# Delta-rule values of a hybrid decoder layer: from channels to tokens by VectorE in squares of 32 and two transfers through DRAM, in place of TensorE transposes

## The chip, the core and the metric

The kernel runs on one core of a Trainium2 chip. The metric is the device time of one execution in microseconds (us), lower is better. Three runs of the kernel before gave 1606.45, 1606.53 and 1606.76 us; their median is 1606.53 us.

Engines in the profile: PE is TensorE, PEld its weight loads, DVE VectorE, ACT ScalarE, POOL GpSimd, SP SyncE. Each engine has one queue that it works off in order; SP issues nearly all DMAs and, being in order as well, stands still while the first DMA in its queue waits for something.

## The reference

One layer for 512 tokens and 1024 channels, all float32: half of a SwiGLU block is added, then a mixer, then half of a second SwiGLU block. The mixer projects its input once and feeds two recurrent branches; the change lies in one of them, the gated delta rule with 8 key heads and 16 value heads:

```python
qkv = jax.nn.silu(causal_short_conv(jnp.concatenate([gq, gk, gv], axis=-1), conv_w))
cq, ck, cv = jnp.split(qkv, [GDN_WIDTH_K, 2 * GDN_WIDTH_K], axis=-1)
...
T = lax.linalg.triangular_solve(eye + A, ...)          # a triangle per chunk and head
u = jnp.matmul(T, v * beta[..., None])
...
v_new = u_c - jnp.einsum('bhtk,bhkv->bhtv', w_c, S)
```

The short convolution runs along the tokens, so it wants a channel per partition and tokens along the free dimension. The chunked rule wants tokens on the partitions: its products sum over tokens, and `beta` is a factor per token. So the values `cv` of each of the 16 value heads, 128 channels by 512 tokens, have to be turned once.

## The kernel before

The span has three stages: the first SwiGLU block (to about 357 us), the mixer (to about 1192 us), the second block and the last norm. All dense products are made on PE with operands split in a high and a low part, three products per tile (`mm3`, L189 to L191). Each 256-KB piece of weights (a slab) comes in by one SP load into one of 3 `raw` buffers; ACT casts the high part (L1754), DVE subtracts for the low part (L1756) and then one of 6 pairs of buffers `whi`, `wlo` holds it until PE has used it.

The mixer is laid down by a planner (`Desk`, L64). Every piece of work is a generator that asks for an engine with an estimated duration (`V`, `A`, `T_`, `S` for DVE, ACT, PE, SP), for a buffer (`get`), for an event (`on`) or lets time pass (`lag`, with the due times of `LAG`). The planner replays these estimates and so decides in which order instructions stand in each engine's queue; on the chip that order is fixed and only semaphores count. The dense products are a thread of their own that fills PE; products of the recurrences get PE in between. PSUM has two accumulators "mm" for dense results, and lanes: "a" and "b" with two buffers, "d" and "e" with one.

What the change and the prediction touch:

- `conv` (L1091): takes two of the six `ta` buffers, drains a dense result from "mm" into `ci` (L1097), works out four taps (ACT L1102, three times DVE L1105) and tanh (ACT L1108); a last DVE instruction (L1113) writes the silu. For q and k the result goes to its tile in another view (n is not 0). For the values (n is 0) it goes to the tile `gvb` or `x` of the head, channels on partitions. Then both `ta` buffers come free.
- `g_w` (L1244): waits for the head's values and its factors, takes lane "e", turns the tile by four PE transposes into PSUM (`ptv`, L1251), and DVE multiplies them by a factor per token on the way back into the same tile (L1253).
- `g_rec` (L1333): the recurrence of a unit, that is of two value heads with one key head, in four chunks of 128 tokens: `pks` (L1374, L1375), DVE adds the value (L1378), `pw` (L1387), DVE (L1392), `pog` (L1401, L1403), DVE updates the state (L1410, L1414).
- `g_b`, a step for each unit: sends diagonal blocks to DRAM (`nb`, four issues, L1222), reads them back spread out (`gfs`, four issues of 128 KB, L1228), loads a start matrix (`hmask`, L1234), and POOL solves small triangles with them (L1240, L1241).
- The inverse of a unit continues on PE, ACT and DVE (`pq`, L1289 to L1320, DVE stream transposes L1265, L1272, L1329), the triangle itself comes from `pgq` (L1189, with DVE L1193 and L1195), the turned output is `pto` (L1445, DVE L1449).
- `loader` (L1696): SP's weight loads. It asks `choose` for the next projection, and where nothing can be loaded yet it asks again after 0.5 us of planned SP time (L1702).

The two loops over the units: 8 units, each with two value heads, so 16 heads v0 to v15, 64 transposes and 16 multiplies.

Of the kernel before, what the change touches and what calls it, by code (L numbers as in the profile page):

```python
# [8 lines left out]
F32 = mybir.dt.float32  # L9
# [3 lines left out]
ALU = mybir.AluOpType  # L13
# [3 lines left out]
P = 128  # L17
T = 512
NT = T // P
D = 1024  # L20
# [28 lines left out]
STAY = (15,)  # L49
CONVS = 7  # L50
SLACK = 0.8
LAG = dict(raw=3.5, gb=6.5, nb=6, m=7, out=5, back=6)
EASE = 2.5
LANES = {"a": 2, "b": 2, "d": 1, "e": 1}

# [632 lines left out]
def mixer(tc, mp, e):  # L688
    nc = tc.nc
    pe, act, dve, pool, sp = nc.tensor, nc.scalar, nc.vector, nc.gpsimd, nc.sync  # L690
    cs, ident, tri, strict, hm, ones, mhalf = (e[k] for k in ("cs", "ident", "tri", "strict", "hm", "ones", "mhalf"))
    uh, ul, rbc, rcols, rcol, rhalf, h = (e[k] for k in ("uh", "ul", "rbc", "rcols", "rcol", "rhalf", "h"))
    psc, dr, dense, slab, wp, mm3, ux, hd, dbg = (
        e[k] for k in ("psc", "dr", "dense", "slab", "wp", "mm3", "ux", "hd", "dbg"))
    wt, wn, wab, wbh, wbg, wo, dta, psd = (e[k] for k in ("wt", "wn", "wab", "wbh", "wbg", "wo", "dtab", "psd"))

    def ps(name, lane="d"):
        return psc.tile([P, T], F32, tag="p" + lane, name=name, bufs=LANES[lane])

    def v3(ap, a):  # L700
        return ap.rearrange("p (a b) -> p a b", a=a)

    def bc(ap, n):

        return ap.unsqueeze(2).to_broadcast([ap.shape[0], ap.shape[1], n])
# [9 lines left out]
    op = [alloc(f"op{i}", 1) for i in range(8)]  # L715
    ta = alloc("ta", TA)
# [3 lines left out]
    for size, names in ((1024, "n2:2 gz:2 fs:1 ut:1"), (512, "kn:3 gm:1 qm:2 gb:2 ln:1 at:4 vb:4 t64:2 on:2"),  # L720
                        (256, "ft:1 tp:1 thg:2 x:1 we:1 s:3 w:1"), (128, "fm:1"), (64, "sm:4")):
        for it in names.split():
            n, b = it.split(":")
# [35 lines left out]
    D = Desk(wx0=1, wx1=1, wx2=1, wx3=1, mm=2, a=2, b=2, d=1, e=1, ta=TA, tm=6, thg=1, raw=RB, w=WB, n2=2, gz=2, fs=1, ut=1, t=3, kn=3, gm=1,  # L759
             qm=2, gb=2, ln=1, mi=3, mt=3, at=4, vb=4, t64=2, on=2, ft=1, x=1, we=1, w_=1, s=3)  # L760
    V = lambda n: ("use", "DVE", 0.21 + 0.001 * n)
    A = lambda n: ("use", "ACT", 0.2 + 0.0009 * n)
    T_ = lambda n: ("use", "PE", n)
    S = ("use", "SP", 0.4)
# [11 lines left out]
    def decays(pab):  # L776
# [74 lines left out]
        sp.dma_start(gtd, gt)  # L851
        yield "lag", LAG["out"]
        D.fire("decays")
# [237 lines left out]
    def conv(k, i, pt, out, n):  # L1091

        yield "get", "ta", 2
        yield *V(512), 1
        ci = ta("ci", (P, T + 32))[:, :T + 3]
        dve.memset(ci[:, :3], 0.0)
        dve.tensor_tensor(ci[:, 3:], pt, rbc, op=ALU.mult)  # L1097
        D.put("mm")
        wc = [cs[:, C_CV + 4 * i + j:C_CV + 4 * i + j + 1] for j in range(4)]
        yield A(512)  # L1100
        y = ta("cy")
        act.activation(y, ci[:, :T], AF.Copy, scale=wc[0])  # L1102
        for j in range(1, 4):
            yield V(550)
            dve.scalar_tensor_tensor(y, ci[:, j:j + T], wc[j], y, op0=ALU.mult, op1=ALU.add)  # L1105
        yield A(512)
        th = ci[:, :T]
        act.activation(th, y, AF.Tanh, scale=0.5)  # L1108
        a, b = (v3(th, n), v3(y, n)) if n else (th, y)
        if k[0] in "qk" and k[1] > 3:  # L1110
            yield "on", ("K", k[1] - 4)
        yield V(512)
        dve.scalar_tensor_tensor(out, a, 1.0, b, op0=ALU.add, op1=ALU.mult)  # L1113
        D.put("ta", 2)
        D.fire(k)

    def g_e(u, st):

# [2 lines left out]
        for i in range(2):  # L1121
# [4 lines left out]
            act.dma_start(gb, gtd[hd_:hd_ + 1].rearrange("o (c b) -> o c b", c=NT).to_broadcast([P, NT, P]))  # L1126
            yield "lag", LAG["gb"]
            a = G["at"][u % 4 * 2 + i]
# [85 lines left out]
    def g_b(u, st):  # L1214
# [4 lines left out]
        for b in range(4):  # L1219
            r = slice(32 * b, 32 * b + 32)  # L1220
            yield S
            sp.dma_start(nb[b].rearrange("s i j -> i s j"), n2[r, :, :, r].rearrange("p a c j -> p (a c) j"))  # L1222
        yield "lag", LAG["nb"]
        yield "on", *([("P", u - 1)] if u else ["m"])
# [9 lines left out]
        sp.dma_start(t, eye4)  # L1234
        yield "lag", LAG["m"]
        for j in range(31):
# [6 lines left out]

    def g_w(u, i, st):  # L1244
        yield "on", ("v", 2 * u + i), ("C", u)
        yield "get", "e", 1
        vb = G["vb"][u % 3 * 2 + i]
        yield T_(Patient(.5))
        pt = ps("ptv", "e")
        for c in range(NT):  # L1250
            pe.transpose(pt[:, c * P:(c + 1) * P], vb[:, c], ident)  # L1251
        yield V(512)
        dve.tensor_tensor(vb, v3(pt, NT), bc(st["c2"][:, :, i], P), op=ALU.mult)  # L1253
        D.put("e")
        D.fire(("W", u, i))

    def g_inv(u, st):
# [75 lines left out]
    def g_rec(u, st):  # L1333
        yield "on", ("I", u), ("W", u, 0), ("W", u, 1), ("N", u), *([("R", u - 2)] if u > 1 else []), \
            *(["more"] if u else [("x", 0), ("we", 0), ("w", 0)])
        kq, kn, at, ut, sm = (st[k] for k in ("kq", "kn", "at", "ut", "sm"))
        vb = G["vb"][u % 3 * 2:u % 3 * 2 + 2]
        hd2 = [slice(i * P, (i + 1) * P) for i in range(2)]
        we, w, x = (G[n][u % 2] for n in ("we", "w", "x"))
        s = None  # L1340
# [27 lines left out]
        for c in range(NT):  # L1368
            pk = None
            if c > 0:  # L1370
                yield "get", "a", 1
                yield T_(.88)
                pk = ps("pks", "a")
                pe.matmul(pk[:, :256], kq[:, c, 0], s, start=True, stop=True)  # L1374
                pe.matmul(pk[:, 256:], kq[:, c, 1], s, start=True, stop=True)  # L1375
                for i in range(2):
                    yield V(150)
                    dve.scalar_tensor_tensor(x[:, hd2[i]], pk[:, hd2[i]], st["c1"][:, c, i:i + 1], vb[i][:, c],  # L1378
                                             op0=ALU.mult, op1=ALU.add)
                xs = [x[:, :P], x[:, P:]]  # L1380
            else:
                xs = [vb[0][:, c], vb[1][:, c]]
            yield "get", "b", 1
            yield T_(.46)
            pw = ps("pw", "b")
            for i in range(2):
                pe.matmul(pw[:, hd2[i]], ut[:, 4 * i + c], xs[i], start=True, stop=True)  # L1387
            D.start((2, u, c, 0), values(c, pw))
            if c < NT - 1:
                for i in range(2):  # L1390
                    yield V(150)
                    dve.tensor_scalar(we[:, hd2[i]], pw[:, hd2[i]], ek[:, c, 2 * u + i:2 * u + i + 1], None,  # L1392
                                      op0=ALU.mult)
            yield "on", ("w", u, c)
            D.put("b")

            yield "get", "b", 1
            yield T_(.9)
            po = ps("pog", "b")
            if c < NT - 1:  # L1400
                pe.matmul(po[:, :256], kn[:, c], we, start=True, stop=True)  # L1401
            for i in range(2):
                pe.matmul(po[:, 256 + i * P:256 + (i + 1) * P], at[i][:, c], w[:, hd2[i]], start=True, stop=True)  # L1403
            D.start((2, u, c, 1), outputs(c, po, pk))
            if c < NT - 1:
                yield "get", "s", 1
                s2 = places["s"]("s", (P, 256))
                if c == 0:
                    yield V(256)
                    dve.tensor_copy(s2, po[:, :256])  # L1410
                else:
                    for i in range(2):
                        yield V(150)
                        dve.scalar_tensor_tensor(s2[:, hd2[i]], s[:, hd2[i]], eend[:, c, 2 * u + i:2 * u + i + 1],  # L1414
                                                 po[:, hd2[i]], op0=ALU.mult, op1=ALU.add)
                    D.put("s")
                s = s2
                D.fire(("s", u, c))
# [8 lines left out]
                                 op0=ALU.mult, op1=ALU.add)  # L1427
# [12 lines left out]
        for i in range(2):  # L1440
            yield "get", "b", 1
            yield T_(Patient(.5))
            pt = ps("pto", "b")
# [9 lines left out]
            if u == 7:  # L1453
# [3 lines left out]
                a, b = so[k] = uh[:, k - 8], ul[:, k - 8]  # L1457
# [158 lines left out]
    G = {"kq": [hv[:, i].rearrange("p (c a b) -> p c a b", c=NT, a=2) for i in range(3)]}  # L1616
    st = [{} for _ in range(8)]
# [78 lines left out]
    def loader():  # L1696
        n = 0
        while todo or gates:
            yield "get", "raw", 1
            x = choose()  # L1700
            while x is None:
                yield "use", "SP", 0.5  # L1702
                x = choose()
            line.append(x)
            D.fire(("f", x))
            D.fire(("line", len(line)))
            for q, src in enumerate(weights(*x)):
                if q:
                    yield "get", "raw", 1
                yield S  # L1710
                raw = wp.tile([P, 512], F32, tag="raw", name="raw", bufs=RB)
                sp.dma_start(raw, src)
                D.start((1, n), maker((x, q), raw))
                n += 1
        for d, q in wbgs:
            yield "get", "raw", 1
            yield S
            raw = wp.tile([P, 512], F32, tag="raw", name="raw", bufs=RB)
            sp.dma_start(raw, wbg[d][:, q * 512:(q + 1) * 512])
            D.start((1, n), maker((("m", d), q), raw))  # L1720
            n += 1
# [175 lines left out]
    for d in range(8):  # L1897
        hr = ta("hr")
        sp.dma_start(hr, hd[d])
        pt = dense(wo[d], KD, lambda k: ms[k])  # L1900
# [78 lines left out]
```

## Time and profile before

| | |
|---|---|
| median of 3 runs | 1606.53 us |
| the profiled execution's span | 1604.7 us |
| median less span | 1.8 us |
| DVE busy | 1145.7 us (71%) |
| ACT busy | 831.0 us (52%) |
| POOL busy | 408.8 us (25%) |
| DMA | 204.91 MB, mean 128 GB/s |
| granted PE clock, 640 to 1060 us | 1.00 |

The profiled execution's own time isn't listed apart from its span; about 1.8 us lie around the span if it ran like the median. A group's row gives the line, engine, operation, out<-in with the shapes, its count, then busy time in us and the mean of one in ns, then the idle time just before it and what ended it. A timeline row gives start and length in us. PE's records overlap: a dense product is shown with 0.39 us, yet the next starts 0.23 us later. So PE's work is read from starts, not from lengths.

### The profile page before, as it was taken

How to read it: one execution, taken by the hardware profiler on the slowest of the kernel's cores; microseconds unless marked ns; L12 is line 12 of the kernel's file. 1: busy time of each engine (PE TensorE's matmuls, PEld its weight loads, DVE VectorE, ACT ScalarE, POOL GpSimd, SP SyncE). 2: the span in 40 equal slices, each digit the busy share in tenths (PEclk: the TensorE clock that was granted, in tenths of full speed). 3: DMA queues.
4: the chain of work that ended last, by engine and by line, in shares of the span. 5: the costliest groups of instructions: out<-in, count | busy, mean ns of one | idle time of the engine just before them, and what ended most of it. 6: DMA issues, size and time to landing. Idle time of an engine off the chain costs nothing.

```text
span 1604.7 us, 29242 instructions
## 1 busy us (share of the span) xinstructions
PE 1593.7 (99%) x10672; PEld 1386.3 (86%) x10672; DVE 1145.7 (71%) x2259; ACT 831.0 (52%) x1872; POOL 408.8 (25%) x725
## 2 busy tenths in 40 slices
PE   9999999999999999999999999999999999999997
PEld 8999998888888888888888888888888899999887
DVE  6888785447787778668788888765545788878433
ACT  5766674332434345456665665554324666667222
POOL 0211212001221221156545556600001121121001
PEclk9999999999999999999999999999999999999998
DMA  5766863332312322443242334445543586686333
GB/s 187 168 162 156 181 160 103 113 117 86 106 47 68 86 92 87 137 135 104 93 125 80 119 107 129 134 136 186 164 142 128 140 183 158 154 187 146 92 91 117
DMA packets 121824, 204.91 MB, mean 128 GB/s; under 512 B 21184, under 2 KB 27072, under 8 KB 121680
## 3 DMA queue, kind: packets, MB, share of 16 engines
q1 hardware_dynamic: 104688, 172.40, 34.3%
q0 software_dynamic: 14400, 26.22, 10.2%
q10 hardware_dynamic: 2592, 4.42, 1.0%
q8 instruction: 84, 1.38, 0.4%
q14 instruction: 60, 0.49, 0.1%
HBM read 188.02 MB, written 14.97 MB: 126 GB/s over the span
## 4 chain that ended last, share of the span: by engine, by line
PE 91%; DMA 3%; issue 3%; DVE 2%; ACT 0%; POOL 0%; POOLq 0%; SPq 0%; DVEq 0%; ACTq 0%
PE pmm L189 19%; PE pmm L191 19%; PE pmm L190 19%; PE px L191 6%; PE px L190 6%; PE px L189 6%; DMA wlo<-w1a 2%; PE pnat L189 2%; PE pnat L191 2%; PE pnat L190 2%; PE pgq L1189 1%; PE pw L1387 1%; PE pog L1403 1%; PE pl L974 1%; PE pd L917 1%
## 5 line engine op out<-in xcount | busy, mean ns | idle before, releaser
L189 PE MATMUL pmm<-uh,whi 128*128 128x512 f32 x879 | 361.3, 411 | 0.0
L191 PE MATMUL pmm<-uh,wlo 128*128 128x512 f32 x879 | 343.0, 390 | 0.0
L190 PE MATMUL pmm<-ul,whi 128*128 128x512 f32 x879 | 341.9, 389 | 0.0
L191 PE MATMUL px<-xs,wlo 128*128 128x256 f32 x1008 | 285.7, 283 | 1.3 <-DMA wlo<-w1a 0.7
L190 PE MATMUL px<-xs,whi 128*128 128x256 f32 x1008 | 285.2, 283 | 0.0
L189 PE MATMUL px<-xs,whi 128*128 128x256 f32 x1008 | 285.2, 283 | 0.0
L1754 ACT CAST whi<-raw 128x512 fp32r<-128x512 f32 x226 | 140.2, 621 | 242.7 <-PE pmm L190 195.2
L1756 DVE TENSOR_TENSOR wlo<-raw,whi 128x512 fp32r<-128x512 f32 x226 | 158.3, 702 | 118.2 <-ACT whi L1754 116.2
L191 PEld LDWEIGHTS pmm<-uh,wlo 128*128 128x128 f32 x879 | 165.0, 188 | 36.1 <-DVE wlo L607 0.2
L191 PEld LDWEIGHTS px<-xs,wlo 128*128 128x128 f32 x1008 | 193.5, 192 | 2.1 <-DMA wlo<-w1a 1.1
L189 PEld LDWEIGHTS px<-xs,whi 128*128 128x128 f32 x1008 | 193.5, 192 | 0.1
L190 PEld LDWEIGHTS px<-xs,whi 128*128 128x128 f32 x1008 | 193.5, 192 | 0.1
L189 PEld LDWEIGHTS pmm<-uh,whi 128*128 128x128 f32 x879 | 165.5, 188 | 30.4
L190 PEld LDWEIGHTS pmm<-ul,whi 128*128 128x128 f32 x879 | 165.7, 189 | 29.5 <-DVE ul L216 0.2
L329 ACT CAST whi<-sw 128x512 fp32r<-128x512 f32 x144 | 87.6, 613 | 92.8 <-DVE sw L366 72.6
L308 DVE TENSOR_TENSOR wlo<-raw,whi 128x512 fp32r<-128x512 f32 x100 | 77.7, 788 | 76.7 <-ACT whi L329 76.3
L329 ACT CAST whi<-raw 128x512 fp32r<-128x512 f32 x104 | 61.2, 592 | 125.6 <-PE pmm L190 92.8
L227 POOL TENSOR_TENSOR acc<-acc,sqt 128x512 f32<-128x512 f32 x18 | 23.4, 1302 | 319.8 <-ACT sqt L225 319.8
L308 DVE TENSOR_TENSOR wlo<-sw,whi 128x512 fp32r<-128x512 f32 x144 | 98.0, 681 | 0.0
L329 ACT CAST whi<-rw 128x512 fp32r<-128x512 f32 (+1 forms) x130 | 79.6, 613 | 26.6 <-PE px L190 13.4
L190 PE MATMUL pmm<-xs,whi 128*128 128x512 f32 (+1 forms) x238 | 89.7, 377 | 0.1
L189 PE MATMUL pmm<-xs,whi 128*128 128x512 f32 (+1 forms) x238 | 89.8, 377 | 0.0
(476 smaller groups left out, 3223.5 us busy)
## 6 DMA issues: line engine op xcount, KB each, us to landing
raw<-wt SPq DMA_DIRECT2D x160, 256.0 KB
rw<-w1b SPq DMA_DIRECT2D x80, 256.0 KB
rw<-w1a SPq DMA_DIRECT2D x74, 256.0 KB
wlo<-w1b POOLq DMA_DIRECT2D x53, 256.0 KB, 4.8
wlo<-w1a POOLq DMA_DIRECT2D x47, 256.0 KB, 5.0
raw<-w2b SPq DMA_DIRECT2D x41, 256.0 KB
raw<-w2a SPq DMA_DIRECT2D x36, 256.0 KB
raw<-wn SPq DMA_DIRECT2D x32, 256.0 KB
```

Source lines behind the costliest of these rows:

```text
L189: pe.matmul(pt, ah, bh, start=first, stop=False)
L190: pe.matmul(pt, ah, bl, start=False, stop=False)
L191: pe.matmul(pt, al, bh, start=False, stop=last)
L227: add.tensor_tensor(acc, acc, s, op=ALU.add)
L308: dve.tensor_tensor(lo, x, hi.bitcast(F32), op=ALU.subtract)
L329: act.copy(hi, x)
L917: pe.matmul(pd[c // 2][:, (c % 2) * 192:(c % 2) * 192 + 192], ke[:, c * P:(c + 1) * P], qq[:, c], start=True, stop=True)
L974: pe.matmul(pl_[s0:s0 + 32, c * 16:(c + 1) * 16], ke[:, c * P + s0:c * P + s0 + 32], qv[:, c, r, :, 1], start=True, stop=True)
L1189: pe.matmul(pq[:, (c % 2) * 256:(c % 2) * 256 + 256], kq[:, c, 0], kq[:, c].rearrange("p a b -> p (a b)"), start=True, stop=True)
L1387: pe.matmul(pw[:, hd2[i]], ut[:, 4 * i + c], xs[i], start=True, stop=True)
L1754: act.copy(hi, raw)
L1756: dve.tensor_tensor(lo, raw, hi.bitcast(F32), op=ALU.subtract)
```

## The change

For the 16 value heads only:

- The last DVE instruction of `conv` writes in place (into `cy`). A new DVE instruction, `turn`, transposes the 16 by 4 squares of 32 by 32 of `cy` into `ci`; tokens then lie on partitions, but only within squares: the four bands of 32 partitions hold bands of channels in place of bands of tokens.
- `bounce` moves the squares: one SP write of 256 KB to a scratch tensor in DRAM, and after it four SP reads of 64 KB each, in pieces of 512 bytes, into the head's tile. The planner books `S` for each issue, and a lag of 2.5 after the write and after the last read. One `ta` buffer comes free after the silu, the other only when the write has landed. The event that tells that the values are there is fired after the last read.
- `g_w` no longer takes lane "e" and has no PE transposes; the multiply reads and writes SBUF in place.
- The recurrence reads the values through a view (channels in another order).
- The loader asks again after 0.2 us in place of 0.5, and with the last priority.

```diff
-LAG = dict(raw=3.5, gb=6.5, nb=6, m=7, out=5, back=6)
+LAG = dict(raw=3.5, gb=6.5, nb=6, m=7, out=5, back=6, turn=2.5)
...
         yield V(512)
-        dve.scalar_tensor_tensor(out, a, 1.0, b, op0=ALU.add, op1=ALU.mult)
-        D.put("ta", 2)
+        if n:
+            dve.scalar_tensor_tensor(out, a, 1.0, b, op0=ALU.add, op1=ALU.mult)
+            D.put("ta", 2)
+        else:
+            dve.scalar_tensor_tensor(y, a, 1.0, b, op0=ALU.add, op1=ALU.mult)
+            yield V(512)
+            turn(th, y)
+            D.put("ta")
+            yield from bounce(f"vn{i}", th, out, "ta")
         D.fire(k)
+
+    def turn(out, x):
+        dve.transpose(out.rearrange("p (f c j) -> p c f j", f=4, c=NT), x)
+
+    def bounce(name, x, out, tag=None):
+        yield S
+        scr = dr.tile([P, T], F32, name=name)
+        sp.dma_start(scr, x)
+        yield "lag", LAG["turn"]
+        if tag:
+            D.put(tag)
+        for f in range(4):
+            yield S
+            sp.dma_start(out[32 * f:32 * f + 32].rearrange("p (r a) -> p r a", r=4),
+                         scr.rearrange("(r i) (f a) -> f i r a", i=32, f=4)[f])
+        yield "lag", LAG["turn"]
...
     def g_w(u, i, st):
         yield "on", ("v", 2 * u + i), ("C", u)
-        yield "get", "e", 1
-        vb = G["vb"][u % 3 * 2 + i]
-        yield T_(Patient(.5))
-        pt = ps("ptv", "e")
-        for c in range(NT):
-            pe.transpose(pt[:, c * P:(c + 1) * P], vb[:, c], ident)
+        vb = G["vb"][u % 3 * 2 + i].rearrange("p r (c j) -> p r c j", c=NT)
         yield V(512)
-        dve.tensor_tensor(vb, v3(pt, NT), bc(st["c2"][:, :, i], P), op=ALU.mult)
-        D.put("e")
+        dve.tensor_tensor(vb, vb, st["c2"][:, :, i].unsqueeze(1).unsqueeze(3).to_broadcast([P, 4, NT, 32]), op=ALU.mult)
...
-        vb = G["vb"][u % 3 * 2:u % 3 * 2 + 2]
+        vb = [x.rearrange("p r (c j) -> p c r j", c=NT) for x in G["vb"][u % 3 * 2:u % 3 * 2 + 2]]
...
-                    dve.scalar_tensor_tensor(x[:, hd2[i]], pk[:, hd2[i]], st["c1"][:, c, i:i + 1], vb[i][:, c],
+                    dve.scalar_tensor_tensor(v3(x[:, hd2[i]], 4), v3(pk[:, hd2[i]], 4), st["c1"][:, c, i:i + 1], vb[i][:, c],
...
-                yield "use", "SP", 0.5
+                yield "use", "SP", 0.2, 20
```

By the program's own count PE has 64 matrix instructions less (9273 to 9209), DVE 16 more (2261 to 2277), SP 80 more DMAs; ACT and POOL have as many as before. Since the planner replays the whole mixer with the new requests, the order in all queues shifts from the first value head on: dense results, triangles, recurrence steps and weight loads stand in another order in the changed program, and that order can be read from the program.

## The prediction

> **What bounds the kernel now.** First the page: busy time by engine, and the chain that ended last.
>
> ```profile
> PE 1593.7 (99%) x10672; PEld 1386.3 (86%) x10672; DVE 1145.7 (71%) x2259; ACT 831.0 (52%) x1872; POOL 408.8 (25%) x725
> ```
> ```profile
> PE 91%; DMA 3%; issue 3%; DVE 2%; ACT 0%; POOL 0%; POOLq 0%; SPq 0%; DVEq 0%; ACTq 0%
> ```
>
> PE is never idle for long and carries 91% of the chain. So a PE instruction removed is worth its place in the queue, and anything that makes PE wait is a loss in full. Next the second half of the mixer (the view of windows: stretch and length in us, busy of PE, PEld, DVE, ACT, POOL, granted PE clock, DMA share, GB/s), and who waits there (the view of waits for 640 to 1060 us: us in total, times, longest).
>
> ```profile
> 840.00:1060.00 220.00, 220.00 (x1479) 183.07 (x1479) 182.27 (x406) 131.91 (x396) 124.35 (x289) 1.00 0.36 113
> ```
> ```profile
> DVE wlo L1756 <- ACT whi L1754: 47.6, 54, 2.9
> ```
> ```profile
> SPq L1712 <- DVE wlo L1756: 196.0, 75, 5.8
> ```
>
> From 840 to 1060 us PE is full and DVE is busy 83%. What DVE idles is mostly (47.6 us from 640 to 1060) a wait for the high part of the next slab, which ACT casts when PE lets go of a weight buffer. So DVE can't run ahead of PE: each slab conversion ties it to a PE product, and its small cushion is what an added DVE microsecond eats. SP idles 196.0 us; it has time for 80 more issues.
>
> **What goes away on PE.** 64 transposes in 16 runs of four.
>
> ```profile
> L1251 PE MATMUL ptv<-sq,gvb 128*128 128x128 f32 x48 | 7.3, 275 | 0.0
> ```
> ```profile
> 670.52 0.39 PE L191 MATMUL pmm<-oh,wlo 128*128 128x512 f32 x1
> 670.75 0.60 PE L1251 MATMUL ptv<-sq,gvb 128*128 128x128 f32 x4
> 671.11 0.48 PE L189 MATMUL pmm<-oh,whi 128*128 128x512 f32 x1
> 671.42 0.39 PE L190 MATMUL pmm<-oh,whi 128*128 128x512 f32 x1
> ```
>
> A record lasts 275 ns, but records overlap. From 670.75 to 671.42 PE started four transposes and one dense product; the dense one alone takes 670.75 - 670.52 = 0.23. So a run of four costs 0.67 - 0.23 = 0.44 us, and 16 runs 7.0. [...] I take the 7.0 of the starts.
>
> **What comes on DVE.** Sixteen `turn`s of 128x512. The trace has stream transposes of other sizes:
>
> ```profile
> L1272 DVE STREAM_TRANSPOSE h<-x 32x256 f32<-32x256 f32 x8 | 3.5, 435 | 0.2
> ...
> L1265 DVE STREAM_TRANSPOSE x<-gln 128x256 f32<-128x256 f32 x3 | 2.1, 701 | 0.0
> ...
> L1329 DVE STREAM_TRANSPOSE gt<-gut 32x128 f32<-32x128 f32 x6 | 1.8, 303 | 0.9 <-ACT gut L1302 0.7
> ```
>
> From 128 to 256 elements 132 ns are added, so 512 would take 435 + 2 x 132 = 0.70 us; by the row with 128 partitions, whose writes are scattered more finely, twice 0.701 = 1.4. The squares of `turn` are written in runs of 32 as in L1272: I take 0.70, and keep 1.4 as the far end. That is 11 us of DVE work in a stage of some 400; the multiply stays (SBUF in place of PSUM as source, I take the same 0.68 as for L1253 below). The silu in place is the same instruction. None of this costs time by itself; what it costs is decided at the places where PE waits for DVE. Those depend on the new order.
>
> **Where the new order makes PE wait.** I went through the order of the changed program and summed, for each PE instruction that waits for DVE, PE's work and DVE's work since a common PE product. DVE's work goes by these rows (of 357 to 1192 us, each form by itself), less overlap:
>
> ```profile
> L1756 DVE TENSOR_TENSOR wlo<-raw,whi 128x512 fp32r<-128x512 f32 x222 | 155.7, 702 | 112.5 <-ACT whi L1754 110.5 <-PE pw L1387 0.6
> L1105 DVE SCALAR_TENSOR_TENSOR cy<-ci,cs,cy 128x512 f32<-128x512 f32 x96 | 72.6, 760 | 4.5 <-ACT cy L1102 3.1
> ...
> L1097 DVE TENSOR_TENSOR ci<-pmm,rbc 128x512 f32<-128x512 f32 x32 | 22.0, 687 | 5.1 <-PE pmm L191 4.9
> ...
> L1449 DVE SCALAR_TENSOR_TENSOR on<-pto,cs,ggz 128x512 f32<-128x512 f32 x12 | 8.9, 745 | 0.3 <-PE pto L1445 0.3
> ...
> L1113 DVE SCALAR_TENSOR_TENSOR gvb<-ci,cy 128x512 f32<-128x512 f32 x12 | 8.4, 702 | 0.9 <-ACT ci L1108 0.8
> ...
> L1193 DVE TENSOR_TENSOR gm<-pgq,sq 128x256 f32<-128x256 f32 x16 | 6.7, 417 | 2.5 <-PE pgq L1189 2.5
> ...
> L1378 DVE SCALAR_TENSOR_TENSOR gx<-pks,sm,gvb 128x128 f32<-128x128 f32 x18 | 5.4, 341 | 1.1 <-PE pks L1375 1.0
> ```
> ```profile
> L1754 ACT CAST whi<-raw 128x512 fp32r<-128x512 f32 x226 | 140.2, 621 | 242.7 <-PE pmm L190 195.2 <-issue 21.4 <-PE pnat L191 8.4
> ```
> ```profile
> 864.10 0.69 DVE L1756 TENSOR_TENSOR wlo<-raw,whi 128x512 fp32r<-128x512 f32 x1 [0.53 <-ACT whi L1754]
> 864.71 0.68 DVE L1253 TENSOR_TENSOR gvb<-ptv,sm 128x512 f32<-128x512 f32 x1
> ```
> ```profile
> 859.84 0.59 PE L1374 MATMUL pks<-s,h 128*128 128x256 f32 x2
> 860.27 0.59 PE L1375 MATMUL pks<-s,h 128*128 128x256 f32 x2
> ...
> 873.13 0.68 PE L1312 MATMUL pq<-gut,gn 64*64 64x64 f32 x16
> 873.74 1.13 PE L1189 MATMUL pgq<-h 128*128 128x256 f32 x4
> ```
>
> DVE's neighbours overlap by 0.08 us (864.10 to 864.71 for a length of 0.69). The last two fences are from the timelines of DVE and PE (start, length). By starts, half a `pks` takes 0.43 us and the whole 0.86, `pgq` of the same shape 0.86 too; a level of the inverse (`pq`) takes 0.6, and `pto`, `ptk` and `pw` 0.44 like the four transposes above.
>
> Place 1, triangle of unit 5 and inverse of unit 3. Both accumulators "mm" are full with k6 and q6, and no `ta` buffer is free for their drain, since value convolutions hold theirs longer (`turn`, then until the write has landed). So PE has no dense product: `pgq`, `pto`, `pq`, `pto`, `pq`, `pgq` are 0.86 + 0.44 + 0.6 + 0.44 + 0.6 + 0.86 = 3.8 us. The next dense product waits for a drain (L1097) on DVE behind, counted from the last dense product: its tail 0.16 (0.39 less 0.23), cast 0.621, conversion 0.702, tap 0.760, `on` 0.745, the multiply of v7 0.68, two halves of the triangle at 0.417, two transposes at 0.303, `on` 0.745, silu 0.702, `turn` 0.70, drain 0.687: 7.9, less 11 overlaps of 0.08 7.1. With 0.1 allowed for the semaphore, PE waits 7.1 + 0.1 - 3.8 = 3.4.
>
> Place 2, unit 4's recurrence: the drain stands behind 0.16, 0.621, 0.702, four of 0.341, 0.701, four of 0.435, `turn` 0.70, drain 0.687: 6.7, less 12 overlaps 5.8; PE has 12 dense products, `pks`, `ptk` and `pw`, 12 x 0.23 + 0.86 + 0.44 + 0.44 = 4.5. Wait: 5.8 + 0.1 - 4.5 = 1.4.
>
> Place 3, unit 5: `pks` is followed at once by `pw` and the dense product: 0.86 + 0.44 = 1.3 us of PE work against 0.16, 0.621, 0.702, four of 0.341, 0.70, 0.687: 4.2, less 7 overlaps 3.7. Wait: 3.7 + 0.1 - 1.3 = 2.5.
>
> Together 7.3, if a wait is not made good later: PE is never idle for want of anything else, so nothing behind it catches up. With a `turn` of 1.4 it is 2.1 more. Lower ends are 3.0, 0.7 and 1.9, since the sums rest on mean durations and the cast may find its buffer earlier. In the old order I find no such place: there the longest stretch without a dense product is 2.2 us, and the accumulator of the next one is free by then.
>
> At three more places in the neighbourhood of the first, PE would be late by 1 to 2 us by the same sums; these are the same lag, already paid at place 1, and I add nothing.
>
> **Waits for the bounce.** DVE's multiply (W) now waits for DMA, and every slab conversion and drain stands behind it. Between `turn` and W of one head lie, by the new order, 6 to 12 us of DVE's time: least for v14 (5.8), v4 (6.1), v8 (6.5), v2 (7.0); 8.4 for v7 (summed as above, waits for PE included). What the bounce takes:
>
> ```profile
> 1593.44 2.67 DMA yT<-rw
> ```
> ```profile
> 664.54 2.74 SPq L1228 DMA_DIRECT2D gfs<-nb  x4
> 667.39 0.40 SPq L1234 DMA_DIRECT2D gft<-hmask  x1
> ```
> ```profile
> 674.18 0.25 POOL L1240 TENSOR_TENSOR fm<-gfs,gft 128x31 f32<-128x31 f32 x1 [5.71 <-DMA gft<-hmask]
> ```
>
> A write of 256 KB takes 2.67 us. With reads like it, issued 0.4 apart, a bounce takes 2.67 + 3 x 0.4 + 2.67 = 6.5. Behind a burst of four `gfs` a transfer landed 674.18 - 667.39 = 6.8 after its issue, and for v0, v5, v7, v9 and v13 such a burst stands between the write and its reads or just ahead of the write: 2.67 + 1.2 + 6.8 = 10.7, plus up to 3 us in which SP itself issues the burst. That the burst counts at all comes from SP's order: the reads stand behind `gfs` there, and each of SP's DMAs also waits for the one eight places ahead of it. So DVE is held by 0 to 4 us at a W. Most of it is covered: behind W of v0 stand conversions that PE needs much later, and it may be 5 us late before PE's `pgq` of unit 1 notices. Not covered are v7, whose W is part of place 1, and v8, v9 right behind. I take 1 us each for v7, v8 and all others together: 3, with 0 and 7 as ends. [...]
>
> **Edits at nothing.** Weight loads behind a bounce on SP: SP waits for buffers 196.0 us in this stretch, and its 80 new issues are 80 x 0.4 = 32 us; a slab is converted several slabs ahead of its use. If that cover were gone, PE would wait for `wlo`, up to the 6.5 of a bounce. The recurrence's view (L1378): same sizes, 0.341. Lane "e": nobody else asks for it. The loader's shorter question changes only the planned order, which the sums above already read.
>
> **Sum.** -7.0 + 7.3 + 3.0 = +3.3. The profiled span of 1604.7 becomes 1608.0, and with 1.8 around it the time is **1609.8**, against a median of 1606.53.
>
> **Rivals.** (a) The bounces land in time: -7.0 + 7.3 = +0.3, 1606.8. For it: 6.5 against leads of 6 to 12. Against: the bursts. (b) Faster: DVE makes up its lag before PE gets there, because the accumulators come free earlier than I count, and only the removed transposes count: 1606.5 - 7.0 = 1599.5. It decides at place 1: if the drain ends within 3.8 us of the last dense product, the stall is gone. For it: before, PE hardly waits though DVE is 83% busy. Against: 7.1 of listed DVE work. (c) Reads late at most heads: holds at 7, with `turn` at 1.0 (0.9 more at three places): -7.0 + 8.2 + 7 = +8.2, 1614.7. For it: the 6.8 behind a burst; against it: 196 us of SP's idle time and a DMA share of 0.36. That PE keeps its transposes is excluded by the program. [...]
>
> **How the numbers follow.** Forecast 0.44, (a) 0.34, (b) 0.06, (c) 0.16. A measurement can tell about 0.2%, 3.2 us, from no change: faster is below 1603.3, slower above 1609.7. The forecast lies near this border; between 1607.5 and 1612.5 it is flat with a little more above, and I give it 0.36 slower, 0.08 same. So slower 0.36 + 0.16 = 0.52, same 0.34 + 0.08 = 0.42, faster 0.06. The range: all of (a) with smaller stalls (3.0, 0.7, 1.9: 1605.1), and (c) without its last microsecond: 1604.5 to 1614.5. The forecast's own range is 1607.5 to 1612.5.
>
> **What would show it.** Right: no `ptv`; idle PE before a dense product ended by DVE's drain `ci`, about 3.4, 1.4 and 2.5 us, near 875, 905 and 1000 us; `turn` at 0.70; DVE idle before L1273 ended by the reads, above all for v0, v7, v8, v9. Wrong: PE busy at 99% without such gaps (rival b); gaps, but DVE not late at W (a); a `turn` near 1.4; late slabs, with PE waiting for `wlo` or ACT for `raw`.

## The result, and the profile after

Five runs of the changed kernel have a median of 1618.74 us (1618.5 to 1620.31), five of the kernel before on the same chip 1606.53 us (1605.87 to 1606.76). The ratio is 1.0079, with a 95% interval of 1.0067 to 1.0091: the change costs some 12 us. The profiled execution's span is 1617.5 us against 1604.7. The forecast had the sign, but 1618.74 lies above its range (1604.5 to 1614.5).

The page of the changed kernel, busy time by engine and the chain that ended last:

```profile
PE 1593.9 (99%) x10608; PEld 1380.8 (85%) x10608; DVE 1156.3 (71%) x2275; ACT 831.3 (51%) x1872; POOL 413.0 (26%) x725
...
PE 82%; DMA 8%; issue 6%; POOL 2%; DVE 1%; SPq 1%; ACT 1%; POOLq 0%; DVEq 0%; ACTq 0%
```

PE has 64 instructions less and is busy just as long; 9 points of the chain have gone from PE, most of them to DMA (5) and to issue (3). The view of windows for the second half of the mixer (columns as in the prediction), and the view of waits of PE from 357 to 1200 us (in total, times, longest), where the kernel before has no row at all:

```profile
840.00:1060.00 220.00, 209.44 (x1320) 170.33 (x1319) 178.23 (x391) 125.87 (x368) 124.63 (x290) 0.98 0.44 132
```
```profile
PE pgq L1214 <- DVE gqm L1220: 4.7, 2, 3.7
PE pmm L189 <- DVE ci L1097: 2.3, 2, 1.3
PE pw L1406 <- DVE x L1397: 2.2, 2, 1.6
PE pq L1331 <- ACT gut L1321: 1.1, 1, 1.1
PE pks L1393 <- DVE s L1429: 1.1, 2, 0.8
PE pmm L189 <- DVE zg L1513: 0.8, 1, 0.8
```

So PE now waits ten times, 12.2 us together, nine of them for DVE. In this stretch it is idle for 10.6 us and gets a mean clock of 0.98 where it had 1.00: two different losses. What DVE waits for itself (waits from 640 to 1100 us) and what its new instructions cost (groups, 357 to 1192 us):

```profile
DVE gvb L1273 <- DMA gvb<-vn: 18.9, 7, 6.0
```
```profile
L1126 DVE STREAM_TRANSPOSE ci<-cy 128x512 f32<-128x512 f32 x16 | 11.3, 705 | 0.3
...
L1273 DVE TENSOR_TENSOR gvb<-gvb,sm 128x512 f32<-128x512 f32 x12 | 8.8, 729 | 18.9 <-DMA gvb<-vn 18.9
```

DVE stands for 18.9 us at the multiply of seven heads because the four reads haven't landed. Place 1 of the prediction, from the timelines of PE, DVE and SP and from the chain (start, length; in brackets the idle time before and what ended it):

```profile
877.61 0.68 PE L1331 MATMUL pq<-gut,gn 64*64 64x64 f32 x16 [1.13 <-ACT gut L1321]
881.97 2.08 PE L1214 MATMUL pgq<-h 128*128 128x256 f32 x4 [3.68 <-DVE gqm L1220]
883.93 0.79 PE L189 MATMUL pmm<-uh,whi 128*128 128x512 f32 x1
884.52 0.63 PE L190 MATMUL pmm<-ul,whi 128*128 128x512 f32 x1
884.95 0.63 PE L191 MATMUL pmm<-uh,wlo 128*128 128x512 f32 x1
...
886.72 0.39 PE L191 MATMUL pmm<-uh,wlo 128*128 128x512 f32 x1
```
```profile
879.00 0.69 DVE L1273 TENSOR_TENSOR gvb<-gvb,sm 128x512 f32<-128x512 f32 x1 [2.55 <-DMA gvb<-vn]
```
```profile
862.35 2.67 SPq L1253 DMA_DIRECT2D gfs<-nb  x4
...
866.67 0.33 SPq L1132 DMA_DIRECT2D vn<-ci  x1
...
872.49 1.27 SPq L1138 DMA_DIRECT2D gvb<-vn  x3
...
874.28 0.43 SPq L1138 DMA_DIRECT2D gvb<-vn  x1
```
```profile
865.89 0.72 DVE ci L1126
866.67 5.76 DMA vn<-ci
874.28 4.60 DMA gvb<-vn
879.00 0.69 DVE gvb L1273
```

Read the last fence from the top: v7's `turn` ends at 866.6, its write takes 5.76 us (the yT write of the prediction took 2.67), then come SP's four issues, then 4.60 us until the last read has landed. That is 12.4 us from `turn` to multiply. DVE has nothing else that it may do before it, waits 2.55, and PE's second `pgq` waits 3.68 for DVE. Behind it records of PE last 0.63 in place of 0.39 and dense products start 0.43 apart in place of 0.23: the clock is halved, to 0.50 from 878.80 to 885.63 us. The dense product at 883.93 doesn't wait for its drain; at place 1 the idle time stands before `pq` (for ACT) and `pgq` (for DVE), where the prediction had it before the dense product. The windows show the clock here and at place 3:

```profile
882.00:886.00 4.00, 4.00 (x21) 2.46 (x23) 3.73 (x8) 1.01 (x2) 3.37 (x9) 0.55 0.34 131
1011.00:1015.00 4.00, 3.67 (x10) 2.90 (x11) 2.66 (x7) 1.03 (x2) 0.00 (x0) 0.62 0.43 122
```

The clock's loss in a window is (1 less the clock) times PE's busy time. Summed over windows of one microsecond, the changed kernel loses 3.6 us to the clock in the mixer and the kernel before none.

To see where the 12 us arise, the start of every dense product was compared with that of the same number in the kernel before. The delay grows by 12.2 us within the mixer and by 0.6 outside it. "Mixer" with a sign below is this growth, from the one profiled execution of each kernel. For order_only below that execution took 1609.24 us, the longest of its ten, and for no_bounce 1613.17, the longest of its five; their mixers go with these times and not with the medians.

### The profile page after: what moved, and what is told of

Its sections match the earlier page's. It is cut to its first block, busy times and chain, and to the rows that moved or that the text cites. A ratio compares the mean times of both kernels' runs of the same rounds, so it can differ in the third digit from the quotient of the medians.

```text
span 1617.5 us, 29307 instructions
## 1 busy us (share of the span) xinstructions
PE 1593.9 (99%) x10608; PEld 1380.8 (85%) x10608; DVE 1156.3 (71%) x2275; ACT 831.3 (51%) x1872; POOL 413.0 (26%) x725
## 4 chain that ended last, share of the span: by engine, by line
PE 82%; DMA 8%; issue 6%; POOL 2%; DVE 1%; SPq 1%; ACT 1%; POOLq 0%; DVEq 0%; ACTq 0%
PE pmm L189 18%; PE pmm L190 17%; PE pmm L191 17%; PE px L191 5%; PE px L190 5%; PE px L189 5%; DMA wlo<-w1b 3%; DMA wlo<-w1a 2%; PE pnat L189 2%; PE pnat L191 2%; PE pnat L190 2%; PE pgq L1214 1%; DMA gvb<-vn 1%; PE pw L1406 1%; DMA vn<-ci 1%
```

## The experiments

Theory: the removed transposes are worth about 7 us; the new order, the `turn` and the waits for the bounce make DVE late at a few places; each place costs PE its wait and, as at places 1 and 3 of the changed kernel, a stretch at half clock behind it. Rivals: DVE's added work costs time wherever it stands; the traffic of the bounce slows other transfers; the transposes were never worth 7 us. The kernel before ran with each of the four groups of experiments and had medians of 1606.33, 1606.55, 1605.77 and 1606.35 us.

### Without the transfers, and without the turn

The order of the changed kernel is kept; the values don't get into the layout that the recurrence wants, all else is computed.

`no_bounce`: the `turn` writes straight to the head's tile, and the 80 DMAs are left out.

```diff
-            turn(th, y)
+            turn(out, y)
...
-        scr = dr.tile([P, T], F32, name=name)
-        sp.dma_start(scr, x)
+        pass
...
-            sp.dma_start(out[32 * f:32 * f + 32].rearrange("p (r a) -> p r a", r=4),
-                         scr.rearrange("(r i) (f a) -> f i r a", i=32, f=4)[f])
+            pass
```

> The changed kernel in its own order, all 16 turns kept, but the 80 transfers through DRAM are not issued: turn writes straight into the head's tile, so the values stay mixed up between the bands (that part of the computation is left out). Theory A (the loss is DVE held at the multiply W until the reads land, 18.9 us of idle DVE in 7 waits, and what stands behind it): PE's idle time in the mixer falls from about 12 us to the three places that were forecast from DVE's own work (3.4, 1.4, 2.5), the clock doesn't drop, time 1606 to 1610. Theory B (the new order of the instructions alone costs the time): 1615 or more. Theory C (turn's 11.3 us of DVE work costs it): 1615 or more.

`order_only`: the `turn` is left out as well, and the silu writes to the tile. What is left of the change is the order, and the transposes that are gone.

```diff
-            dve.scalar_tensor_tensor(y, a, 1.0, b, op0=ALU.add, op1=ALU.mult)
+            dve.scalar_tensor_tensor(out, a, 1.0, b, op0=ALU.add, op1=ALU.mult)
             yield V(512)
-            turn(th, y)
+            pass
```

> As before, and the turns aren't issued either: the silu writes the head's tile as in the kernel before, so what is left of the change is the new order without the 64 transposes on PE (the values aren't turned to tokens: left out). Theory A: the forecast places each lose one turn (0.7 us), -7.0 + 2.7 + 0.7 + 1.8 = -1.8, 1603 to 1606. Theory B (order alone): 1613 or more. Theory C: 7 to 12 us below the run with turns.

`no_turn`: all DMAs, but no `turn`; the write takes the silu itself.

```diff
-            turn(th, y)
...
-            yield from bounce(f"vn{i}", th, out, "ta")
+            yield from bounce(f"vn{i}", y, out, "ta")
```

> The changed kernel in its own order with all 80 transfers, but no turn on DVE: the write takes the silu itself (no squares are transposed: left out). Theory A (late reads): DVE still waits at W, 1613 to 1617, since 0.7 less of DVE work before each write only moves the write. Theory C (turn's work on DVE): 1607 or less.

Measured, with the mixer's growth, PE's listed waits and the loss by the clock:

| | median, us | ratio (95%) | mixer | PE waits | clock |
|---|---|---|---|---|---|
| order_only | 1607.42 | 1.0007 (0.9998 to 1.0016) | +1.7 | 4.0 | 3.0 |
| no_bounce | 1612.41 | 1.0037 (1.0022 to 1.0051) | +6.5 | 6.6 | 5.0 |
| no_turn | 1619.55 | 1.0084 (1.0069 to 1.0099) | +12 | 13.4 | 2.7 |
| the changed kernel | 1618.74 | 1.0079 (1.0067 to 1.0091) | +12.2 | 12.2 | 3.6 |

With the order alone the kernel is already back at the time of before: what the transposes gave is spent. With the `turn` it is 5.0 us more, with the transfers 6.3 more again. But the terms don't add: without the `turn` the transfers cost 1619.55 - 1607.42 = 12.1. Without the `turn` the multiply still waits 17.9 us for the reads, nearly as long as in the changed kernel (18.9), and PE waits 13.4 in place of 12.2 (waits of DVE, 640 to 1100 us, in no_turn):

```profile
DVE gvb L1273 <- DMA gvb<-vn: 17.9, 7, 5.9
```

So the wait for the bounce is decisive in this order, and DVE's work of 11.3 us adds nothing next to it. Why PE waits longer without the `turn` wasn't followed up; v7's write took 6.46 us there in place of 5.76, and the wait at 1022 us 3.39 in place of 1.61.

All three runs lie above what was expected by theory A, by 1.4 us (order_only), 2.4 (no_bounce) and 2.6 (no_turn). Theory A of no_bounce had the clock stay full; the three lose 2.7 to 5.0 us to it. order_only and no_bounce have no transfers, so the three places that the order makes are enough to halve the clock.

The waits of PE in no_bounce, from 640 to 1100 us:

```profile
PE pmm L189 <- DVE ci L1097: 3.2, 3, 1.3
PE pq L1331 <- ACT gut L1321: 1.1, 1, 1.1
PE pgq L1214 <- DVE gqm L1220: 1.1, 1, 1.1
PE pmm L189 <- DVE zg L1513: 0.6, 1, 0.6
PE pw L1406 <- DVE x L1397: 0.6, 1, 0.6
```

By its timeline these are 1.13, 1.10 and 0.84 at place 1, 1.32 at place 2, 0.61 and 1.01 at place 3, and 0.62 at 865 us. The waits on the three places that the order makes, 6.0 us, are there without any DMA.

### What the transposes are worth

`before_no_pt`: the kernel before in its own order, without its 64 transposes; the multiply takes the unturned tile.

```diff
-            pe.transpose(pt[:, c * P:(c + 1) * P], vb[:, c], ident)
+            pass
...
-        dve.tensor_tensor(vb, v3(pt, NT), bc(st["c2"][:, :, i], P), op=ALU.mult)
+        dve.tensor_tensor(vb, vb, bc(st["c2"][:, :, i], P), op=ALU.mult)
```

> The kernel before in its own order, but without the 64 transposes on PE: the multiply takes the head's tile itself (values aren't turned: left out). Price by starts: 16 x 0.44 = 7.0 us, 1599.5. Price by the length of the records (275 ns each): 17.6 us, 1589. If PE's order has no room for it elsewhere (a later wait takes the place): nearer 1606.

Measured: 1601.96 us, ratio 0.9974 (0.9963 to 0.9984); mixer -5.4, with 0.6 us of new PE waits and no clock lost. That is 6.0 without the waits, 0.37 us a run of four. In a better order (lag9_bare, below), where PE never waits, the same 64 transposes less give -7.0, which is 0.44 a run; how much of the difference is that order's own wasn't separated. Both are far from 17.6, which 275 ns a record would give.

### What a wait does to the clock

`stall13`, `stall20`, `stall5`, `stall7`: the kernel before, and memsets of about 0.64 us on DVE ahead of one drain, 13, 20, 5 or 7 of them. It computes what before does.

```diff
+        for _ in range(13 if k == ("q", 1) else 0): dve.memset(ci[:, 3:], 0.0)
         dve.tensor_tensor(ci[:, 3:], pt, rbc, op=ALU.mult)
```

> The kernel before with 13 memsets of 128x512 put on DVE ahead of the drain of q1, at a place where the clock is full: they hold DVE for some 4 to 6 us and so make PE wait once. Theory clock (a wait of PE costs more than itself, since TensorE's clock is halved after it): with 2 us or more idle, the stretch after it shows a granted clock under 0.9 and dense products 0.43 us apart for some 3 us, and the mixer ends later than the idle time alone. Without: products 0.23 us apart right after the wait.

> As stall13 with 20 memsets: a longer wait of PE. Theory clock: about 2 us on top of the idle time, as one stretch of half clock, not more than in stall13 in proportion to the wait. Without: the loss grows with the idle time alone.

> The kernel before with 5 memsets of 0.64 us on DVE ahead of one drain (q1); its output is that of before. 13 of them made PE wait 7.4 us and 20 made it wait 11.9, so about 0.9 us is slack: PE should wait about 2.3 us once. Theory A (the clock halves only after a wait of more than about 3 us): no dense product of the mixer starts 0.43 after its neighbour, and the mixer is 2.3 us longer. Theory B (a wait of about 2 us is enough): products 0.43 us apart for about 4 us behind it, mixer 4.3 us longer.

> The same with 7 memsets: PE should wait about 3.6 us once. Theory A (over about 3 us): clock halved for about 4 us, mixer 5.6 us longer. Theory B (2 us are enough): the same. If neither this nor the run with 5 halves the clock, the waits of the kernel after did not halve it by their length, but by what stood around them.

Each makes PE wait once (`po` for `hs`, which DVE works out behind the memsets). One run each:

| | PE's wait, us | mixer | more than the wait | time, us |
|---|---|---|---|---|
| stall5 | 2.0 | +3.8 | 1.8 | 1609.72 |
| stall7 | 3.3 | +5.2 | 1.9 | 1610.41 |
| stall13 | 7.4 | +9.4 | 2.0 | 1615.66 |
| stall20 | 11.9 | +13.8 | 1.9 | 1620.66 |

PE's timeline in stall5:

```profile
622.15 0.38 PE L1023 MATMUL po<-v,ah 128*128 128x128 f32 x2
624.53 0.61 PE L1025 MATMUL po<-hs,qp 128*128 128x128 f32 x2 [2.00 <-DVE hs L1034]
624.93 0.63 PE L1028 MATMUL pu<-v,hkn 128*128 128x128 f32 x2
625.22 0.77 PE L189 MATMUL pmm<-uh,whi 128*128 128x512 f32 x1
625.79 0.63 PE L190 MATMUL pmm<-ul,whi 128*128 128x512 f32 x1
626.22 0.63 PE L191 MATMUL pmm<-uh,wlo 128*128 128x512 f32 x1
...
628.27 0.39 PE L1025 MATMUL po<-hs,qp 128*128 128x128 f32 x2
```

One wait of 2.0 us is enough here: dense products lie 0.43 apart behind it, and some 3.6 us after PE starts again its records are back at 0.39. The price is the wait, plus about 0.2 (a record lasts 0.16 longer than the distance to its neighbour, and a wait lays that bare), plus 1.6 to 1.9 by the clock, whatever the length of the wait from 2.0 to 11.9. So theory A of stall5 fell, and B holds at this place.

But the length of a wait doesn't decide alone. In no_turn a lone wait of 3.39 us left the clock at full speed:

```profile
1022.70 0.75 PE L1406 MATMUL pw<-x,x 128*128 128x128 f32 x4 [3.39 <-DVE x L1397]
1023.20 0.48 PE L189 MATMUL pmm<-uh,whi 128*128 128x512 f32 x1
1023.51 0.40 PE L190 MATMUL pmm<-ul,whi 128*128 128x512 f32 x1
1023.74 0.39 PE L191 MATMUL pmm<-uh,wlo 128*128 128x512 f32 x1
```

The view of windows, cut in steps of 3.41 us from where the half clock of the same run begins (columns as before, PE's busy time first, the clock third from the end). First no_turn, then order_only, stall5 and stall20:

```profile
1017.66:1021.07 3.41, 1.65 (x8) 0.99 (x6) 0.51 (x1) 1.56 (x4) 1.81 (x7) 1.00 0.15 52
1021.07:1024.49 3.42, 1.79 (x10) 1.59 (x11) 3.26 (x9) 2.14 (x9) 2.79 (x9) 1.00 0.44 134
```
```profile
872.25:875.66 3.41, 2.15 (x55) 1.56 (x53) 3.35 (x7) 2.50 (x7) 2.78 (x9) 1.00 0.61 219
875.66:882.49 6.83, 5.86 (x27) 4.35 (x28) 5.02 (x11) 2.98 (x8) 5.73 (x15) 0.50 0.11 41
```
```profile
621.33:624.75 3.42, 1.43 (x9) 1.06 (x8) 2.97 (x8) 1.07 (x4) 0.00 (x0) 1.00 0.00 0
624.75:628.16 3.41, 3.41 (x12) 2.83 (x12) 2.11 (x4) 1.09 (x5) 0.00 (x0) 0.50 0.28 82
```
```profile
621.49:624.90 3.41, 1.59 (x8) 1.14 (x7) 2.46 (x6) 0.11 (x1) 0.00 (x0) 1.00 0.00 0
624.90:628.31 3.41, 0.00 (x0) 0.00 (x0) 2.54 (x6) 0.00 (x0) 0.00 (x0) 1.00 0.00 0
```

In these runs the stretches at half clock last 3.41 us (stall5, place 3 of the changed kernel), 6.83 (order_only, place 1) or 10.24 (stall20), and where a run has two they begin a whole number of 3.41 us apart (878.80 and 1011.92 us in the changed kernel, 39 times; 878.74 and 1008.44 in no_bounce, 38 times). They don't begin with the wait: in stall5 PE stands from 622.53 to 624.53 and the half clock begins at 624.75; at place 1 it begins at 878.80, 0.5 us after the wait of 3.68 has begun. The 2.00 us of stall5 lie within one of the steps, and the next has a clock of 0.50. The 3.39 of no_turn fall on two, 1.76 and 1.63; the lone 1.33 (at 916 us) and 1.61 (at 1022 us) of the changed kernel, behind which the clock stayed at 1.00 too, fall on two as well. At place 3 the 0.62 and 1.01 lie in one step, and the clock was 0.50 in the next. At place 1 the step before 878.80 has 1.64 us of idle time, 1.13 of them the wait for ACT.

Idle time within a step doesn't decide alone either: in order_only 1.26 us were followed by a clock of 0.50, in stall20 1.82 us by a step at 1.00. What else decides isn't shown; the four stall runs varied the length of a wait and nothing beside it.

### The same change in another order

`lag6`, `lag7`, `lag9`: the changed kernel, whole, with another lag for the planner. It books 6, 7 or 9 us for the write and again for the reads, and lays the queues accordingly.

```diff
-LAG = dict(raw=3.5, gb=6.5, nb=6, m=7, out=5, back=6, turn=2.5)
+LAG = dict(raw=3.5, gb=6.5, nb=6, m=7, out=5, back=6, turn=9)
```

> As lag7 with LAG turn=6, about 14 us from turn to W: another order. Theory A: DVE's waits before W under 4 us; by the sums PE is late by 1.1 and 2.1 us at two places; 1602 to 1606. Theory B: 1612 or more.

> The changed kernel with one number: LAG turn=7 in place of 2.5, so that the planner books about 16 us from turn to the multiply W, where the bounce took 6.4 us alone and 12.4 to 14.8 us behind a gfs burst. Theory A (the loss is made by an order that was planned with a bounce of about 7 us): DVE's idle time before W falls from 18.9 to under 3 us, and by the sums of DVE's work PE is late by 1.1 us at most at one place: the 5.4 us that the missing transposes gave in the mixer remain for the most part, 1601 to 1604. Theory B (turn's DVE work or the DMA traffic costs the time in any order): 1612 or more.

> The changed kernel with the planner's lag for the two transfers at 9 in place of 2.5; it computes the reference. With 7 the ratio was 0.9986 and the mixer 2.9 us shorter than in the kernel before, with 6 it was 1.0014. Theory (the order decides, and a good order is one in which no multiply of the values waits for its reads and no drain stands behind them): a replay of this order's PE, DVE and ACT work gives PE about 1 us less idle than with 7, so the time is 1602 to 1605, with DVE's waits for vn under 3 us and no PE wait over 1.2 us. Rival (more lag holds the ta buffers longer on the planner's clock and so pushes the drains back, as it does in the kernel after): PE waits for drains again and the time is 1606 or more.

`lag9_bare`: lag9 without the `turn` and the DMAs, edited as order_only is.

> The order of lag9 with its turns and its 80 DMAs left out (the silu goes straight to the head's tile, so the values stay unturned; the multiply and all else is there). lag9 itself was 0.9978 of the kernel before, its mixer 4.7 us shorter. Theory (in a good order both the turn and the transfers are hidden, so what lag9 gains is the 64 transposes and nothing else counts): the time is within 1.5 us of lag9's 1602.3 and the mixer 4.7 to 5.6 us shorter than before's. Rival (the turn and the transfers still cost several us there, and the order itself is faster than before's): the mixer is 7 us or more shorter and the time 1600 or less.

| | median, us | ratio (95%) | mixer | PE waits |
|---|---|---|---|---|
| lag6 | 1608.49 | 1.0014 (1.0004 to 1.0023) | +1.9 | 6.0 |
| lag7 | 1604.17 | 0.9986 (0.9977 to 0.9996) | -2.9 | 2.1 |
| lag9 | 1602.27 | 0.9978 (0.9969 to 0.9987) | -4.7 | 1.6 |
| lag9_bare | 1599.92 | 0.9959 (0.9946 to 0.9973) | -7.0 | none |

The waits of lag9 from 357 to 1200 us, those of PE and the one of DVE that is for a transfer of the values, and its window:

```profile
PE pw L1406 <- DVE x L1397: 1.2, 1, 1.2
PE pmm L189 <- DVE ci L1097: 0.4, 1, 0.4
```
```profile
DVE tg L1498 <- DMA vn<-ci: 3.0, 1, 3.0
```
```profile
840.00:1060.00 220.00, 218.75 (x1476) 181.00 (x1475) 188.56 (x412) 134.48 (x397) 127.42 (x285) 1.00 0.45 138
```

The same `turn`s and the same 80 transfers, 16.5 us faster than in the order of the changed kernel, and faster than before. No multiply waits for its reads; the clock stays at 1.00. DMA share and GB/s are no lower than in the changed kernel (0.44 and 132), so traffic as such isn't the cause. In lag9_bare PE doesn't wait at all, and the mixer is shorter by the 7.0 of the prediction's first term (6.0 in the old order, so up to 1 us of it may be this order's own). The expectation there was that turn and transfers are hidden in a good order; half of that held. They cost 1602.27 - 1599.92 = 2.35 us (by the mixers 7.0 - 4.7 = 2.3), of which the 1.2 and 0.4 are seen as waits. Nor does more lag always help: lag6, between 2.5 and 7, is slower than lag7 by 4.3 us, with PE waits of up to 1.5 us at other places; it missed its expectation (1602 to 1606), lag7 the upper end of its own (1604) by 0.2.

The rivals: DVE's added work costs 2.35 us or less in the order of lag9 and 5.0 in that of no_bounce, so it has no fixed price; the traffic is excluded by lag9; the transposes are worth 6.0 to 7.0 where PE doesn't wait.

The loader's edit needs no run: the kernel before with 0.2 and the last priority, and the changed kernel with 0.5, give the same instructions in the same order on every engine as without that edit. It does nothing.

## Why the prediction was wrong

Two terms failed. The sum puts what the clock does after a wait at nothing, and it cost 3.6 us; the holds were taken at 3.0 and measured 5.6, or 6.1 with the tails below. The forecast of the span was 1608.0 and the span is 1617.5, 9.5 more: 3.6 by the clock, 3.1 by the holds, 0.4 by the places (7.7 with tails in place of 7.3), and 2.4 that stay open, 1.8 in the mixer and 0.6 outside it. The split between places and holds takes no_bounce as the kernel without holds.

- **What goes, -7.0**: right or nearly. -7.0 in the order of lag9_bare, -6.0 in the old order without the two small waits there (-5.4 with them).
- **`turn` at 0.70, its far end 1.4**: right, 0.705. The multiply is a little slower than taken, 0.729 in place of 0.68, and so is the silu in place, 0.729 in place of 0.702.
- **The three places, +7.3**: right in place and nearly in size. Without transfers 3.07, 1.32 and 1.62 (forecast 3.4, 1.4, 2.5), 6.0 together. Place 3 was counted 0.9 too high; which of its summed durations was too long was not followed up. The 0.1 allowed for the semaphore was my estimate: nine of the ten waits of the changed kernel end 0.05 to 0.06 us after the instruction that PE waits for, one 0.15 after. At place 1 the lag was split on three waits, and the forecast mechanism, a dense product that waits for its drain, has 0.84 of the 3.07. Small slips of the text: the list of place 2 gives 5.7 and so 1.3, the row of L1754 counts the whole span (its mean is the same), and the range's upper end lies 0.2 below rival (c), not a microsecond.
- **The holds, +3.0, ends 0 and 7**: a step that failed, in size. PE waits 12.2 against 6.6 without transfers: 5.6. By places that is 1.7 at place 1 (v7), 1.61 at 1022 us (v13), 0.99 for v0, 0.84 at 778 us and 0.4 at two others. Forecast were 6.5 for a clear bounce and 10.7 plus up to 3 behind a burst of `gfs`. The clear one is borne out at v2, the shortest: its `turn` ended at 721.71, the write was issued at 721.78 and the reads from 724.27, and the multiply came at 729.57 without a wait. It isn't general: v8, v14 and v15, with no burst near, held their multiplies by 1.19, 1.49 and 1.32, which came 10.6, 7.7 and 9.2 after `turn`. v8's last read was issued 4.7 after its first, behind a weight load on SP. Behind a burst it was 12.4 for v7: both halves were slow, and I had put the longer time on the reads alone and left the write at 2.67. v1 wasn't on the list of five and was held by 4.11, since its write stood in SP's queue behind v0's reads: `turn` ended at 668.77, the write was issued at 673.77. For v0 the prediction said that it may be 5 us late before `pgq` of unit 1 notices; it was 5.99 late, and that `pgq` waited 0.99. At 778 us a step of the recurrence waited 0.84, which no_bounce doesn't show; its path wasn't followed. One hold I didn't price at all: v13's write kept its `ta` buffer for 6.59 us, ACT's tap stood 7.35 for it, the slab's cast behind it was late, then DVE, then PE by 1.61.
- **What comes after a wait: not in the sum**: the other failed step. The 7.3 were summed as waits alone, each at its own length. At places 1 and 3 the clock was halved: 3.6 us. no_bounce, with the places alone, loses 5.0 by it. The trace of before had no such wait in the mixer, so no price for it either; its 1.00 in the quoted window stood beside a PE that was never idle there (220.00 of 220.00 us).
- **The tail of a record**: about 0.16 for each of the ten waits, 1.6. The sums of the three places were made by starts and have it in them; for the holds it is missing.
- **Edits at nothing**: right. PE never waits for `wlo`, and the loader's edit changes nothing.

The sum as measured: -7.0 + 12.2 (waits) + 1.6 (tails) + 3.6 (clock) = 10.4, against 12.2 in the mixer. 1.8 us are left open there (order_only and no_bounce leave 0.9 and 0.8 by the same sum), and 0.6 outside it. With the -6.0 of the old order in place of -7.0, order_only and no_bounce come out within 0.2, and 0.8 is left for the changed kernel; so the first term may be 1 us too large in this order, which is argued from the sums only. The rival that came nearest is (c), reads late, at 1614.7; its `turn` of 1.0 was wrong, its holds of 7 nearer than mine, and it too lacked the clock. That the bursts of `gfs` are what slows the bounce is argued from the trace: the writes of v7, v9 and v13, behind a burst, took 5.76, 5.23 and 6.59 us, and seven others that SP waited for, with none just ahead, 2.01 to 3.74. A kernel without these bursts wasn't run.

## What to carry to other kernels

Added work on an engine that is off the critical path cost little by its busy time here (`turn` and transfers together 2.35 us in lag9, for 11.3 us of `turn`); it cost at the few places where the order leaves no slack between two engines, and there a wait of 2.0 us cost PE 3.8, with its clock at 0.50 behind it (stall5). When a step is replaced by one with a longer latency, tell the planner that latency as the loaded chip has it (12 to 15 us here behind a burst, booked at 2.5 twice) before the idea itself is judged: one constant moved this kernel from 1.0079 to 0.9978. Try more than one value, since lag6 gave 1.0014. And price a round trip through DRAM with both of its halves at what such a transfer takes in the busy stretch.

## What the hardware showed

- PE's granted clock in the mixer was 1.00, and 0.50 in stretches of 3.41 us (stall5), 6.83 (order_only) and 10.24 (stall20). The two of the changed kernel begin 39 times 3.41 us apart, the two of no_bounce 38 times. It halved after a single wait of 2.0 us (stall5), and did not after a lone one of 3.39 (no_turn). A step of 3.41 us with 1.26 us idle was followed by half clock (order_only), one with 1.82 idle was not (stall20). Behind one wait the stretch at half clock cost 1.6 us after a wait of 2.0 (stall5) and 1.8 after one of 11.9 (stall20).
- In the changed kernel a write of 256 KB to DRAM took 2.0 to 3.7 us with no burst of `gfs` just ahead (seven writes), and 5.2 to 6.6 behind such a burst (three). The last reads of 64 KB took 4.60 and 5.15 behind one for v7 and v0, 2.7 for v9, and 2.5 to 4.0 for v1, v8, v14 and v15.
- A DVE transpose in squares of 32 of 128x512 float32 took 0.705 us (the 16 of the changed kernel), within the range of the other DVE instructions of that size in the prediction's rows (0.68 to 0.76).
